# Inverse and chain of a recurrence, by group of four heads, in a hybrid attention layer

## The chip, the core and the metric

The kernel runs on one core of a Trainium2 chip. The metric is the device time of one execution in microseconds. A core has TensorE (PE, with its weight loads PEld), VectorE (DVE), ScalarE (ACT), GpSimd (POOL) and SyncE (SP), which here only issues DMAs. Each engine works through its own list of instructions strictly in order and waits where a semaphore isn't there yet.

## The reference

One layer, D_MODEL 1024, 1024 positions. A normed input is multiplied with `w_in`; the product is split into a part for latent attention (4 heads), a part for an RWKV-7 recurrence (8 heads of 64) and a gate z. Cut to the recurrence:

```python
def step(S, inp):
    r_t, w_t, k_t, v_t, kk_t, a_t = inp
    sa = jnp.einsum('bhvk,bhk->bhv', S, -kk_t)
    S = (S * w_t[:, :, None, :] + sa[..., None] * (kk_t * a_t)[:, :, None, :]
         + v_t[..., None] * k_t[:, :, None, :])
    return S, jnp.einsum('bhvk,bhk->bhv', S, r_t)
...
_, ys = lax.scan(step, S0, xs)
y = jnp.moveaxis(ys, 0, 1)          # then a group norm per head, scale, bias and a bonus term
...
y_cat = jnp.concatenate([y_mla, y_rw], axis=-1) * jax.nn.silu(z)
h = h + rmsnorm(y_cat @ w_out[l], norm_post_g[l])
```

## The kernel before

The positions go in two halves h of 512, and a half in 8 chunks (NCH) of 64 for the recurrence. Within a chunk the recurrence is written with matrices: a head needs the inverse of a 64 x 64 unit triangular matrix per chunk, and then a chain of small matmuls carries the state from chunk to chunk. The heads form two groups g of four; cb counts pairs of heads (128 columns), so that blocks 0 and 1 belong to group 0, and 2 and 3 to group 1.

A string, PROGRAM, lists the stages. A letter is a stage, its digits are the half and the block or group:

- A: load x, norm it, transpose it and split it into uH and uL (L181 scales, L188 transposes, L192 and L193 split). X: the inputs of the low-rank weights.
- P h cb: projections r, k, v (L221, with weights split by L201 on ScalarE and L209 or L211 on GpSimd), and the factors of the recurrence (L322 and L329 write LS).
- E h cb: the unit matrices (L372, masked by L376 and L377 into AB and LS; L386, L399, L407).
- I: the inverse. C: the chain. N and G: group norm and outputs (L522 to L542).
- Z, Y: projections of the gate z (also L221, L602), stored to zs. M, T: attention's input. B: rope tables. U, K, J, Q, S: attention and the output product (L814 and L862 scores, L894, L942 output).

The stages are written in this order. A scheduler then places every instruction in its engine's list by a model of the times; buffers in rotation (`ch` 2, `wk` 2 and `pj` 4 in PSUM; AB, LS, BK and SV one per group, shared by both halves) and data set the waits. BEHIND holds X0 and B back until the named stage's last instruction.

The inverse of a half works on 128 blocks of 32 x 32 (two groups, four heads, two diagonal blocks, eight chunks), one on each partition. The unit matrices go to `sa` in DRAM (L395) and come back block by partition (L423). For each of 31 columns two VectorE instructions (L430, L432) eliminate, up to 256 elements wide. The inverse and its transpose (L433) go out by two stores (L434, L435) and come back in the matmuls' layout by 20 loads (L442, L446, L449). Two small matmul stages fill the off-diagonal block (pF at L459, pG at L466, copied by L460, L467, L468).

The chain takes 8 steps a half, each for both groups: matmuls L486 (state times LS), L497 (inverse), L503 (new state) and L493 and L509 (output), with copies L488, L499 and L513 on ScalarE, L500 and the sum L506 on VectorE, and the decayed state SD (L490) on GpSimd.

Of the kernel before, what the change touches and what calls it, by code (L numbers as in the profile page):

```python
# [12 lines left out]
ALU = mybir.AluOpType  # L13
# [8 lines left out]
NCH = HALF // CH  # L22
# [23 lines left out]
def layer(tc, x, pos, w_in, w_out, w_uq, w_ukv, vecs, w2, a2, consts, post_g, out):  # L46
# [17 lines left out]
    with tc.tile_pool(name="sb", bufs=1) as cp, \  # L64
# [65 lines left out]


PROGRAM = (
    "A0 X0 Z00 P00 E00 Z01 P01 E01 Z02 P02 E02 P03 E03 I0 C0 N00 G00 N01 G01 M0 Z03 Z04 Z05 Y06 T0 A1 B X1",
    "P10 E10 Z10 P11 E11 Z11 P12 E12 P13 E13 I1 C1 N10 G10 N11 G11 M1 Z12 T1 Z13 Z14 Z15 Z16 Z17 U K J Q0",
    "Q1 Q2 Q3 S",
)


BEHIND = {"X0": "A0", "B": "I0"}


def recurrence(tc, E):
    nc = tc.nc
    V, S, G, PE, SP = nc.vector, nc.scalar, nc.gpsimd, nc.tensor, nc.sync
    alloc, bc = E["alloc"], E["bc"]
    vec, omm, oka, hka, nkk, hwa, hln, plast, Sst = (
        E[k] for k in ("vec", "omm", "oka", "hka", "nkk", "hwa", "hln", "plast", "Sst"))
# [4 lines left out]
    P1, pj, wk, chp = E["cp"], E["pj"], E["wk"], E["chp"]  # L152
# [4 lines left out]
    ev = (slice(0, 64), slice(64, 128))  # L157
    le = [(l, e) for l in range(2) for e in range(2)]
# [251 lines left out]
        S.copy(SV[0:64, 0::2, 1, :], pv[0:64, :, 64:128])  # L410
        V.tensor_copy(SV[0:64, 1::2, 1, :], pv[64:128, :, 64:128])

    def inverse(h, gt):


        sa = gt["sa"]
        sx = alloc(E["dp"], (2, 2, 2, 2, NCH, 32, 32), f"sx{h}")
        st = alloc(E["dp"], (2, 2, 2, 2, NCH, 32, 32), f"st{h}")
        rows = "g e b l c i j -> (g e b l c) i j"
        XA = alloc(P1, (128, 2, 1024), "XA")  # L420
        X = XA[:, 0].rearrange("p (i c) -> p i c", c=32)
        At = XA[:, 1].rearrange("p (i c) -> p i c", c=32)
        SP.dma_start(At, sa.rearrange(rows))  # L423
        G.memset(XA[:, 0], 0.0)
        G.memset(XA[:, 0, 0::33], 1.0)
        for j in range(31):
            n, w = 31 - j, j + 1
            tmp = alloc(P1, (128, 256), "tmp")
            t3 = tmp[:, 0:n * w].rearrange("p (n w) -> p n w", w=w)
            V.tensor_tensor(t3, bc(At[:, j, j + 1:32].unsqueeze(2), (128, n, w)),  # L430
                            bc(X[:, j, 0:w].unsqueeze(1), (128, n, w)), ALU.mult)
            V.tensor_tensor(X[:, j + 1:32, 0:w], X[:, j + 1:32, 0:w], t3, ALU.add)  # L432
        V.tensor_copy(At, X.rearrange("p i c -> p c i"))  # L433
        SP.dma_start(sx.rearrange(rows), X)  # L434
        SP.dma_start(st.rearrange(rows), At)  # L435
        FX = alloc(P1, (128, 2, 4, NCH, 32), "XA")
        for g in range(2):
            AB = gt["g"][g]["AB"]
            X1, X2T = FX[:, g, 0:2], FX[:, g, 2]
            for e in range(2):  # L440
                p0 = e * 64
                SP.dma_start(X1[p0:p0 + 32].rearrange("p l c j -> p (l c) j"),  # L442
                             sx[g, e, 0].rearrange("l c i j -> i (l c) j"))
                for l in range(2):
                    q = l * 2 + e
                    SP.dma_start(X2T[q * 32:q * 32 + 32], st[g, e, 1, l].rearrange("c i j -> i c j"))  # L446
                for b in range(2):
                    p0 = e * 64 + b * 32
                    SP.dma_start(AB[p0:p0 + 32, :, :, b * 32:b * 32 + 32].rearrange("p l c j -> p (l c) j"),  # L449
                                 st[g, e, b].rearrange("l c i j -> i (l c) j"))  # L450
        for g in range(2):
            AB = gt["g"][g]["AB"]
            X1, X2T, F = FX[:, g, 0:2], FX[:, g, 2], FX[:, g, 3]
            pF = chp((128, NCH, 32))
            for c in range(NCH):
                for l, e in le:
                    q = l * 2 + e
                    r = slice(e * 64, e * 64 + 32)
                    PE.matmul(pF[q * 32:q * 32 + 32, c], AB[r, l, c, 32:64], X1[r, l, c], start=True, stop=True)  # L459
            V.tensor_copy(F, pF)  # L460
            for l in range(2):
                pG = chp((128, NCH, 32))
                for c in range(NCH):
                    for e in range(2):
                        q = slice((l * 2 + e) * 32, (l * 2 + e) * 32 + 32)
                        PE.matmul(pG[e * 64:e * 64 + 32, c], F[q, c], X2T[q, c], start=True, stop=True)  # L466
                end = V.tensor_copy(AB[0:32, l, :, 32:64], pG[0:32])  # L467
                S.copy(AB[64:96, l, :, 32:64], pG[64:96])  # L468
        return end

    def chain(h, gt):

        for g in range(2):
            for e in range(2):
                G.tensor_copy(gt["g"][g]["SV"][ev[e], 0, e], Sst[ev[e], 2 * g:2 * g + 2])
        parts = [tuple(gt["g"][g][k] for k in ("LS", "BK", "AB", "SV")) +
                 (Sst[:, 2 * g:2 * g + 2], gt["Dg"][:, 2 * g:2 * g + 2]) for g in range(2)]
        for c in range(NCH):

            pY = wk((128, 2, 2, 64))  # L480
            pcs = [chp((128, 3, 2, 64)) for _ in range(2)]
            Rs = [alloc(P1, (128, 2, 64), "Rs", bufs=2) for _ in range(2)]
            SD = [alloc(P1, (128, 2, 64), "SD", bufs=2) for _ in range(2)]
            for (LS, BK, AB, SV, St, Dg), pc, R_, D_ in zip(parts, pcs, Rs, SD):
                for l, e in le:
                    PE.matmul(pc[ev[e], 0, l], LS[:, l, c, e, 0:64], SV[:, c, e, l], start=(l == 0), stop=False,  # L486
                              skip_group_check=True)
                S.copy(R_, pc[:, 0])  # L488
                for e in range(2):
                    G.tensor_tensor(D_[ev[e]], SV[ev[e], c, e], bc(Dg[ev[e], :, c:c + 1], (64, 2, 64)), ALU.mult)  # L490
            for g, (LS, BK, AB, SV, St, Dg) in enumerate(parts):
                for l, e in le:
                    PE.matmul(pY[ev[e], g, l], LS[:, l, c, e, 64:128], SV[:, c, e, l], start=(g == 0 and l == 0), stop=False,  # L493
                              skip_group_check=True)
            for (LS, BK, AB, SV, St, Dg), pc, R_ in zip(parts, pcs, Rs):
                for l, e in le:
                    PE.matmul(pc[ev[e], 1, l], AB[ev[e], l, c, 0:64], R_[ev[e], l], start=False, stop=False,  # L497
                              skip_group_check=True)
                S.copy(SV[ev[0], c, 0], pc[ev[0], 1])  # L499
                V.tensor_copy(SV[ev[1], c, 1], pc[ev[1], 1])  # L500
            for (LS, BK, AB, SV, St, Dg), pc, D_ in zip(parts, pcs, SD):
                for l, e in le:
                    PE.matmul(pc[ev[e], 2, l], BK[:, l, c, e], SV[:, c, e, l], start=False, stop=True, skip_group_check=True)  # L503
                for e in range(2):
                    dst = SV[ev[e], c + 1, e] if c + 1 < NCH else St[ev[e]]
                    V.tensor_tensor(dst, pc[ev[e], 2], D_[ev[e]], ALU.add)  # L506
# [102 lines left out]
    lora, xx, gts, cqs, made = {}, {}, {}, {}, {}  # L609
# [29 lines left out]
def attention(tc, E):  # L639
# [92 lines left out]
    def op_k():  # L732
# [348 lines left out]
```

## Time and profile before

| | |
|---|---|
| three runs | 775.58, 780.02, 776.13 us; median 776.13 |
| profiled execution | 775.78 us |
| its span in the trace | 772.4 us |
| TensorE busy | 689.6 us (89%) |
| VectorE busy | 454.0 us (59%) |
| ScalarE, GpSimd busy | 345.8 us (45%), 331.1 us (43%) |
| mean granted clock of TensorE | 0.933 |

The profile page gives busy times, 40 slices of the span with the busy share of each engine and the granted clock in tenths, the DMA queues, the chain of work that ended last, and the costliest groups of instructions with the idle time before them and what ended it. Times in it are of one execution.

### The profile page before, as it was taken

Reading aid. Unit: us, or ns where it says so; the run is one execution under the profiler, and the core shown is the slowest. Engines: PE = TensorE matmul, PEld = TensorE weight load, DVE = VectorE, ACT = ScalarE, POOL = GpSimd, SP = SyncE. Lnnn points to the kernel's source line nnn. Section 1 sums busy time; section 2 is a strip of 40 time slices with the busy share of each in tenths; the row PEclk is TensorE's granted clock in tenths of the full one; section 3 lists DMA queues with packets and bytes.
Section 4 is the critical chain, followed back from the end, with each engine's and each line's share of the span. In section 5 each row is a group of like instructions: output and inputs, shape, how many; then the busy total and the mean of one; then the engine's idle time right before and its main releaser. Section 6 shows DMA issues by size and latency. Waiting matters only on the chain.

```text
span 772.4 us, 13874 instructions
## 1 busy us (share of the span) xinstructions
PE 689.6 (89%) x5136; PEld 564.9 (73%) x5136; DVE 454.0 (59%) x943; ACT 345.8 (45%) x875; POOL 331.1 (43%) x478
## 2 busy tenths in 40 slices
PE   2899998999858999859899989498899999899996
PEld 2677786787746777647778867386789988788885
DVE  4466675639829431684755593486777776644233
ACT  6646544428225452524634532332665475632221
POOL 6656555447712455453463652132512247432220
PEclk9899999999958899958999999598999999999998
DMA  6523332543570132252222554501231044253321
GB/s 185 150 80 89 91 81 65 145 122 100 167 158 19 28 109 58 55 116 60 54 68 72 138 157 124 164 15 30 57 75 49 22 126 121 72 169 121 123 81 55
DMA packets 118819, 72.84 MB, mean 94 GB/s; under 512 B 47072, under 2 KB 108256, under 8 KB 118752
## 3 DMA queue, kind: packets, MB, share of 16 engines
q1 hardware_dynamic: 118752, 71.96, 33.2%
q8 instruction: 40, 0.66, 0.3%
q14 instruction: 27, 0.22, 0.1%
HBM read 54.38 MB, written 17.56 MB: 93 GB/s over the span
## 4 chain that ended last, share of the span: by engine, by line
PE 36%; DVE 12%; DMA 4%; ACT 3%; POOL 2%; issue 2%; SPq 2%; DVEq 0%; ACTq 0%; POOLq 0%
PE pj L942 11%; PE pj L221 5%; PE pj L862 4%; PE ch L894 3%; DVE tmp L430 2%; PE pj L814 2%; DVE XA L432 2%; PE wk L883 2%; PE wk L372 1%; PE ch L503 1%; POOL w L211 1%; PE wk L509 1%; ACT wf L870 1%; PE pj L821 1%; DMA XA<-sa 1%
## 5 line engine op out<-in xcount | busy, mean ns | idle before, releaser
L221 PE MATMUL pj<-uH,w 128*128 128x512 f32 x640 | 214.9, 409 | 5.7 <-ACT sg L289 4.8
L211 POOL TENSOR_TENSOR w<-wf,w 128x256 fp32r<-128x256 f32 x168 | 140.0, 864 | 117.9 <-ACT w L201 106.8
L221 PEld LDWEIGHTS pj<-uH,w 128*128 128x128 f32 x640 | 121.8, 193 | 36.1 <-ACT sg L289 5.4
L221 PE MATMUL pj<-uL,w 128*128 128x512 f32 x320 | 129.4, 405 | 0.0
L221 PEld LDWEIGHTS pj<-uL,w 128*128 128x128 f32 x320 | 61.8, 193 | 14.2 <-issue 1.2
L201 ACT CAST w<-wf 128x1024 fp32r<-128x1024 f32 (+1 forms) x50 | 51.3, 1027 | 35.9 <-PE pj L556 17.3
L490 POOL TENSOR_TENSOR SD<-SV,Dg 64x128 f32<-64x128 f32 x64 | 30.0, 468 | 57.2 <-DVE SV L506 47.8
L874 POOL TENSOR_SCALAR wf<-wf,sm 128x128 f32<-128x128 f32 (+7 forms) x32 | 23.8, 747 | 62.2 <-DVE sm L873 45.4
L999 DVE TENSOR_TENSOR LS<-pj,LS 128x512 f32<-128x512 f32 x16 | 11.1, 691 | 45.1 <-ACT cq L998 44.4
L430 DVE TENSOR_TENSOR tmp<-XA 128x31 f32<-128x31 f32 (+15 forms) x62 | 28.1, 454 | 15.1 <-DMA XA<-sa 13.3
L885 ACT CAST BK<-wk 128x512 fp32r<-128x512 f32 (+3 forms) x48 | 22.6, 484 | 29.2 <-PE wk L883 27.4
L894 PE MATMUL ch<-BK,LS 128*128 128x256 f32 (+1 forms) x160 | 33.0, 288 | 0.2 <-ACT BK L885 0.2
L209 POOL TENSOR_TENSOR w<-wf,w 128x224 fp32r<-128x224 f32 x32 | 22.1, 722 | 25.5 <-ACT w L201 15.4
L886 DVE TENSOR_TENSOR AB<-wk,BK 128x512 fp32r<-128x512 f32 (+3 forms) x48 | 26.1, 551 | 8.5 <-ACT BK L885 8.1
L865 DVE TENSOR_REDUCE mx<-pj 128x1 f32<-128x512 f32 (+3 forms) x48 | 26.0, 552 | 8.5 <-PE pj L864 5.6
L870 ACT ACTIVATE wf<-pj,mx 128x512 f32<-128x512 f32 (+3 forms) x48 | 27.9, 588 | 5.2 <-DVE mx L867 5.0
L432 DVE TENSOR_TENSOR XA<-XA,tmp 128x31 f32<-128x31 f32 (+15 forms) x62 | 27.5, 443 | 1.9
L372 PEld LDWEIGHTS wk<-LS,pl 64*128 64x128 f32 x256 | 19.3, 187 | 12.2 <-issue 11.2
L998 ACT ACTIVATE cq<-pj 128x512 bf16<-128x512 f32 x16 | 9.6, 597 | 41.1 <-PE pj L942 41.1
L894 PEld LDWEIGHTS ch<-BK,LS 128*128 128x128 f32 x160 | 26.8, 197 | 0.9 <-ACT BK L885 0.5
L513 ACT COPY SV<-wk 128x128 f32<-128x128 f32 x32 | 6.9, 269 | 45.6 <-PE wk L509 45.6
L372 PE MATMUL wk<-LS,pl 64*128 64x128 f32 x256 | 24.8, 290 | 2.7 <-DVE LS L377 2.3
(337 smaller groups left out, 1668.2 us busy)
## 6 DMA issues: line engine op xcount, KB each, us to landing
wf<-in_w_in_dram SPq DMA_DIRECT2D x42, 512.0 KB, 3.8
zs<-st SPq DMA_DIRECT2D x16, 256.0 KB, 2.5
wf<-in_x_dram SPq DMA_DIRECT2D x8, 512.0 KB, 3.7
out_dram<-LS SPq DMA_DIRECT2D x16, 256.0 KB, 2.0
wf<-in_w_in_dram SPq DMA_DIRECT2D x8, 448.0 KB, 3.5
bvd<-st SPq DMA_DIRECT2D x8, 256.0 KB, 2.0
SV<-bvd SPq DMA_DIRECT2D x16, 128.0 KB, 2.9
yrw<-SV SPq DMA_DIRECT2D x8, 256.0 KB, 3.1
```

The source lines that it names most:

```text
L201: S.copy(wh, wf)
L211: G.tensor_tensor(wl[:, sl], wf[:, sl], wh[:, sl].bitcast(F32), ALU.subtract)
L221: PE.matmul(ps, w_[:, kb], u_[:, kb], start=(n == 0), stop=(n == 23))
L372: PE.matmul(pE[e][:, ci], pl[ev[e], c4 + ci, 1 - e:3 - e].rearrange("p a b -> p (a b)"), LS[ev[e], c4 + ci, e, :], start=True, stop=True)
L430: V.tensor_tensor(t3, bc(At[:, j, j + 1:32].unsqueeze(2), (128, n, w)), bc(X[:, j, 0:w].unsqueeze(1), (128, n, w)), ALU.mult)
L432: V.tensor_tensor(X[:, j + 1:32, 0:w], X[:, j + 1:32, 0:w], t3, ALU.add)
L490: G.tensor_tensor(D_[ev[e]], SV[ev[e], c, e], bc(Dg[ev[e], :, c:c + 1], (64, 2, 64)), ALU.mult)
L862: PE.matmul(s_, l_, r_, start=(n == 0), stop=(n == 4 and b1 < e))
L870: S.activation(pr[:, b0:b1], sc[:, 0:b1 - b0], AF.Exp, bias=mx[:, 0:1], scale=-1.0, accum_out=sm[:, n5:n5 + 1])
L886: V.tensor_tensor(PL[:, b0:b0 + nb, o], pt[:, 0:nb], PH[:, b0:b0 + nb, o].bitcast(F32), ALU.subtract)
L894: PE.matmul(py[:, o], l_, r_, start=(j == 0 and n == 0), stop=(j == nk - 1 and n == 2), skip_group_check=True)
L942: PE.matmul(po[nb], l_, r_[:, ns], start=(k0 == 0 and k == 0 and n == 0), stop=(k0 == 4 and k == 3 and n == 2), skip_group_check=True)
```

## The change

Inverse and chain become stages of a group. I h g follows the group's second block of unit matrices, and C h g follows it; some z projections move between the blocks.

The inverse of a group has only 64 blocks. Each is put on two partitions, one on each half of the 128: the lower 64 hold the even columns of X and the upper 64 the odd ones. A column j then touches w = j // 2 + 1 columns at most on each partition, instead of j + 1. There are 62 elimination instructions per group (L432, L434), so 124 a half, up to 136 elements wide. A group has two loads of `sa` (L425), four stores (L437, L438) and 12 loads (L444, L448, L451). The chain has 16 steps a half, each of one group, and its pY now comes from the `ch` buffers instead of `wk`. After the change pF stands at L458, pG at L466, the chain's matmuls at L482, L490, L493, L498 and L503, SD at L488, its VectorE copy at L496 and sum at L501.

```diff
-    "A0 X0 Z00 P00 E00 Z01 P01 E01 Z02 P02 E02 P03 E03 I0 C0 N00 G00 N01 G01 M0 Z03 Z04 Z05 Y06 T0 A1 B X1",
-    "P10 E10 Z10 P11 E11 Z11 P12 E12 P13 E13 I1 C1 N10 G10 N11 G11 M1 Z12 T1 Z13 Z14 Z15 Z16 Z17 U K J Q0",
+    "A0 X0 Z00 P00 E00 P01 E01 I00 C00 Z01 P02 E02 Z02 P03 E03 N00 G00 I01 C01 N01 G01 M0 Z03 Z04 Z05 Y06 T0 A1 B X1",
+    "P10 E10 Z10 P11 E11 I10 C10 Z11 P12 E12 Z12 P13 E13 N10 G10 I11 C11 N11 G11 M1 Z13 T1 Z14 Z15 Z16 Z17 U K J Q0",
...
-BEHIND = {"X0": "A0", "B": "I0"}
+BEHIND = {"X0": "A0", "B": "I01"}
...
-    def inverse(h, gt):
-        sa = gt["sa"]
-        sx = alloc(E["dp"], (2, 2, 2, 2, NCH, 32, 32), f"sx{h}")
-        XA = alloc(P1, (128, 2, 1024), "XA")
...
-        SP.dma_start(At, sa.rearrange(rows))
+    def inverse(h, g, gt):
+        AB = gt["g"][g]["AB"]
+        sx = alloc(E["dp"], (2, 2, 2, 2, NCH, 32, 16), f"sx{h}{g}")
+        st = alloc(E["dp"], (2, 2, 2, NCH, 16, 2, 32), f"st{h}{g}")
+        XA = alloc(P1, (128, 2048), "XA")
+        X = XA[:, 0:512].rearrange("p (i k) -> p i k", k=16)
+        Xt = XA[:, 512:1024].rearrange("p (k i) -> p k i", i=32)
+        At = XA[:, 1024:2048].rearrange("p (j t) -> p j t", t=32)
+        G.memset(XA[:, 0:512], 0.0)
+        for o in range(2):
+            SP.dma_start(At[ev[o]], gt["sa"][g].rearrange("e b l c j t -> (e b l c) j t"))
+            G.memset(XA[ev[o], 16 * o:512:33], 1.0)
         for j in range(31):
-            n, w = 31 - j, j + 1
+            n, w = 31 - j, j // 2 + 1
...
-        SP.dma_start(sx.rearrange(rows), X)
-        SP.dma_start(st.rearrange(rows), At)
+        V.tensor_copy(Xt, X.rearrange("p i k -> p k i"))
+        for o in range(2):
+            SP.dma_start(st[:, :, :, :, :, o].rearrange("e b l c k i -> (e b l c) k i"), Xt[ev[o]])
+            SP.dma_start(sx[o].rearrange("e b l c i k -> (e b l c) i k"), X[ev[o]])
...
-    def chain(h, gt):
-        for g in range(2):
-            for e in range(2):
-                G.tensor_copy(gt["g"][g]["SV"][ev[e], 0, e], Sst[ev[e], 2 * g:2 * g + 2])
+    def chain(h, g, gt):
+        for e in range(2):
+            G.tensor_copy(SV[ev[e], 0, e], St[ev[e]])
         for c in range(NCH):
-            pY = wk((128, 2, 2, 64))
-            pcs = [chp((128, 3, 2, 64)) for _ in range(2)]
+            pc = chp((128, 3, 2, 64))
+            pY = chp((128, 2, 64))
...
-        "E": op_e, "I": lambda h: inverse(h, gts[h]), "C": lambda h: chain(h, gts[h]),
+        "E": op_e, "I": lambda h, g: inverse(h, g, gts[h]), "C": lambda h, g: chain(h, g, gts[h]),
```

What the scheduler makes of it is seen in the engines' lists. Before, VectorE's list has the chain's first step of half 0 behind the whole inverse and among the rope tables and A1's split; from the last elimination on, with pF's and pG's copies between:

```order
L430 TENSOR_TENSOR tmp_262_1503<-XA_231_1409 128x31
L432 TENSOR_TENSOR XA_231_1409<-XA_231_1409,tmp_262_1503 128x31
L433 COPY XA_231_1409<-XA_231_1409 128x1024
L193 SCALAR_TENSOR_TENSOR uL_20_99<-pj_398_2730,vec_2_65,uH_19_98 128x256 x2
L460 COPY XA_263_1509<-ch_264_1530 128x256
L193 SCALAR_TENSOR_TENSOR uL_20_99<-pj_399_2739,vec_2_65,uH_19_98 128x256
L467 COPY AB_65_323<-ch_265_1564 32x8x32
```

After, VectorE's list at the first step of group 0's chain in half 0; SV_66 and ch_185 are group 0's state and its step, the rows of XA_304 are group 1's inverse, and BK_68 is a unit matrix of E03:

```order
L496 COPY SV_66_324<-ch_185_1026 64x128
L432 TENSOR_TENSOR tmp_305_1902<-XA_304_1896 128x31
L434 TENSOR_TENSOR XA_304_1896<-XA_304_1896,tmp_305_1902 128x31
L432 TENSOR_TENSOR tmp_306_1905<-XA_304_1896 128x30
L434 TENSOR_TENSOR XA_304_1896<-XA_304_1896,tmp_306_1905 128x30
...
L432 TENSOR_TENSOR tmp_309_1914<-XA_304_1896 128x81
L501 TENSOR_TENSOR SV_66_324<-ch_185_1026,SD_188_1034 64x128 x2
L434 TENSOR_TENSOR XA_304_1896<-XA_304_1896,tmp_309_1914 128x27x5
```

The chain's copy and its sum, which stood behind the inverse, now stand in the middle of the next one, four and a half pairs of eliminations apart.

On TensorE, before, E03's unit matrices (wk_219 and wk_220) follow P03's projections directly:

```order
L372 MATMUL wk_219_1330<-LS_67_325,pl_203_1217 128x128
L372 MATMUL wk_220_1331<-LS_67_325,pl_203_1217 128x128
L372 MATMUL wk_219_1330<-LS_67_325,pl_203_1217 128x128
L372 MATMUL wk_220_1331<-LS_67_325,pl_203_1217 128x128
L372 MATMUL wk_219_1330<-LS_67_325,pl_203_1217 128x128
```

After, the same unit matrices (wk_289 and wk_290) in the middle of M0 (L547 to L549); ch_182 is pF of group 0's inverse:

```order
L548 MATMUL pj_376_2382<-w_380_2387,uH_19_98 128x448
L549 MATMUL pj_376_2382<-w_380_2387,uL_20_99 128x448
L372 MATMUL wk_289_1779<-LS_67_325,pl_273_1666 128x128
L458 MATMUL ch_182_952<-XA_181_939,AB_65_323 32x32 x31
L372 MATMUL wk_290_1780<-LS_67_325,pl_273_1666 128x128
L372 MATMUL wk_289_1779<-LS_67_325,pl_273_1666 128x128
L372 MATMUL wk_290_1780<-LS_67_325,pl_273_1666 128x128
```

pF's 32 matmuls (one of them stands earlier, in P03's last projection), which followed A1's transposes, now stand ahead of all but the first of E03's unit matrices.

More of the change, by code (lines that the diff above doesn't have):

```diff
@@ L451, in inverse @@
[L451 to L463, printed above, removed]
-                    for e in range(2):
[L465 to L468, printed above, removed]
@@ new lines, in inverse @@
+        V.tensor_copy(Xt, X.rearrange("p i k -> p k i"))
+        for o in range(2):
+            SP.dma_start(st[:, :, :, :, :, o].rearrange("e b l c k i -> (e b l c) k i"), Xt[ev[o]])
+            SP.dma_start(sx[o].rearrange("e b l c i k -> (e b l c) i k"), X[ev[o]])
+        FX = alloc(P1, (128, 4, NCH, 32), "XA")
+        X1, X2T, F = FX[:, 0:2], FX[:, 2], FX[:, 3]
+        for e in range(2):
+            p0 = e * 64
+            for o in range(2):
+                SP.dma_start(X1[p0:p0 + 32].rearrange("p l c j -> p (l c) j")[:, :, 16 * o:16 * o + 16],
+                             sx[o, e, 0].rearrange("l c i k -> i (l c) k"))
+            for l in range(2):
+                q = l * 2 + e
+                SP.dma_start(X2T[q * 32:q * 32 + 32], st[e, 1, l].rearrange("c k o i -> (k o) c i"))
+            for b in range(2):
+                p0 = e * 64 + b * 32
+                SP.dma_start(AB[p0:p0 + 32, :, :, b * 32:b * 32 + 32].rearrange("p l c j -> p (l c) j"),
+                             st[e, b].rearrange("l c k o i -> (k o) (l c) i"))
@@ new lines, in inverse @@
+        pF = chp((128, NCH, 32))
+        for c in range(NCH):
+            for l, e in le:
+                q = l * 2 + e
+                r = slice(e * 64, e * 64 + 32)
+                PE.matmul(pF[q * 32:q * 32 + 32, c], AB[r, l, c, 32:64], X1[r, l, c], start=True, stop=True)
+        V.tensor_copy(F.rearrange("p c (k o) -> p c o k", o=2), pF.rearrange("p c (o k) -> p c o k", o=2))
+        for l in range(2):
+            pG = chp((128, NCH, 32))
+            for c in range(NCH):
+                for e in range(2):
+                    q = slice((l * 2 + e) * 32, (l * 2 + e) * 32 + 32)
+                    PE.matmul(pG[e * 64:e * 64 + 32, c], F[q, c], X2T[q, c], start=True, stop=True)
+            end = V.tensor_copy(AB[0:32, l, :, 32:64], pG[0:32])
+            S.copy(AB[64:96, l, :, 32:64], pG[64:96])
@@ new lines, in inverse @@
+        return end
+    def chain(h, g, gt):
+        LS, BK, AB, SV = (gt["g"][g][k] for k in ("LS", "BK", "AB", "SV"))
+        St, Dg = Sst[:, 2 * g:2 * g + 2], gt["Dg"][:, 2 * g:2 * g + 2]
+        for e in range(2):
+            G.tensor_copy(SV[ev[e], 0, e], St[ev[e]])
+        for c in range(NCH):
+            pc = chp((128, 3, 2, 64))
+            pY = chp((128, 2, 64))
+            for l, e in le:
+                PE.matmul(pc[ev[e], 0, l], LS[:, l, c, e, 0:64], SV[:, c, e, l], start=(l == 0), stop=False,
+                          skip_group_check=True)
+            Rs = alloc(P1, (128, 2, 64), "Rs", bufs=2)
+            S.copy(Rs, pc[:, 0])
+            SD = alloc(P1, (128, 2, 64), "SD", bufs=2)
+            for e in range(2):
+                G.tensor_tensor(SD[ev[e]], SV[ev[e], c, e], bc(Dg[ev[e], :, c:c + 1], (64, 2, 64)), ALU.mult)
+            for l, e in le:
+                PE.matmul(pY[ev[e], l], LS[:, l, c, e, 64:128], SV[:, c, e, l], start=(l == 0), stop=False,
+                          skip_group_check=True)
+            for l, e in le:
+                PE.matmul(pc[ev[e], 1, l], AB[ev[e], l, c, 0:64], Rs[ev[e], l], start=False, stop=False,
+                          skip_group_check=True)
+            S.copy(SV[ev[0], c, 0], pc[ev[0], 1])
+            V.tensor_copy(SV[ev[1], c, 1], pc[ev[1], 1])
+            for l, e in le:
+                PE.matmul(pc[ev[e], 2, l], BK[:, l, c, e], SV[:, c, e, l], start=False, stop=True, skip_group_check=True)
+            for e in range(2):
+                dst = SV[ev[e], c + 1, e] if c + 1 < NCH else St[ev[e]]
+                V.tensor_tensor(dst, pc[ev[e], 2], SD[ev[e]], ALU.add)
+            for l, e in le:
+                PE.matmul(pY[ev[e], l], AB[ev[e], l, c, 64:128], SV[ev[e], c, e, l], start=False, stop=True,
+                          skip_group_check=True)
+            S.copy(SV[:, c, 0], pY)
```

56 lines of the change are left out of this document (removed).

## The prediction

> **What bounds the kernel now.** I read the page from the top: the busy shares, then the slices of TensorE and its clock, then a table of stretches cut at the hollow slices, and last the waits inside these.
>
> ```profile
> span 772.4 us, 13874 instructions
> PE 689.6 (89%) x5136; PEld 564.9 (73%) x5136; DVE 454.0 (59%) x943; ACT 345.8 (45%) x875; POOL 331.1 (43%) x478
> PE   2899998999858999859899989498899999899996
> PEclk9899999999958899958999999598999999999998
> ```
>
> TensorE bounds the kernel on average, but not everywhere. Three slices have both a low busy digit and a clock digit of 5, and they fall where the inverse and chain of a half begin or end. The table of stretches prices them. Its columns are the window and its length, then for TensorE, its weight loads, VectorE, ScalarE and GpSimd the busy time with the count, then the granted clock.
>
> ```profile
> core 0: us, PE busy (x) PEld busy (x) DVE busy (x) ACT busy (x) POOL busy (x), PEclk, DMA share, GB/s
> 63.00:119.40 56.40, 56.40 (x325) 44.52 (x324) 39.23 (x56) 28.19 (x56) 32.18 (x46) 1.00 0.34 87
> 209.00:256.00 47.00, 33.54 (x469) 25.65 (x468) 25.89 (x69) 18.44 (x47) 14.13 (x23) 0.68 0.42 108
> 324.00:352.00 28.00, 16.63 (x111) 13.94 (x108) 23.20 (x38) 9.44 (x24) 16.89 (x19) 0.57 0.47 109
> 352.00:411.00 59.00, 56.48 (x333) 44.67 (x332) 37.17 (x55) 26.21 (x53) 26.82 (x36) 0.97 0.24 63
> 411.00:482.00 71.00, 67.58 (x455) 54.98 (x456) 41.65 (x89) 27.64 (x71) 33.86 (x51) 0.98 0.46 126
> 482.00:506.00 24.00, 13.68 (x233) 9.94 (x225) 12.75 (x30) 7.95 (x24) 5.41 (x10) 0.57 0.52 147
> 531.00:561.00 30.00, 25.20 (x355) 20.90 (x355) 19.46 (x51) 15.35 (x55) 11.79 (x16) 0.89 0.23 54
> ```
>
> I take as lost what is left of a stretch after busy time times clock, as an estimate: 47 − 33.5 × 0.68 = 24.2 us at the end of half 0, 28 − 16.6 × 0.57 = 18.5 us in half 1's first block, 24 − 13.7 × 0.57 = 16.2 us at half 1's inverse, and 30 − 25.2 × 0.89 = 7.6 us at the end of its chain. Together 66.5 us. The first row is the opposite: over two blocks of projections and unit matrices (P01 to E02, with two z projections) TensorE stood still nowhere, and VectorE was busy 39.2 of 56.4 us. It has 17 us to spare there, and that is the room into which the change puts half an inverse.
>
> What do the hollow stretches wait for? The inverse's DMA round trip, as SyncE's queue shows (start, duration of the issue, line):
>
> ```profile
> 164.10 2.14 SPq L395 DMA_DIRECT2D sa<-AB  x4
> 167.54 0.34 SPq L423 DMA_DIRECT2D XA<-sa  x1
> ...
> 210.15 0.33 SPq L435 DMA_DIRECT2D st<-XA  x1
> 212.84 0.32 SPq L442 DMA_DIRECT2D XA<-sx  x1
> 223.13 0.98 SPq L449 DMA_DIRECT2D AB<-st  x2
> ...
> 483.07 0.97 SPq L449 DMA_DIRECT2D AB<-st  x2
> 484.14 0.91 SPq L589 DMA_DIRECT2D zs<-st  x2
> 488.57 1.81 SPq L713 DMA_DIRECT2D cq<-cTd  x4
> ```
>
> Then how long L449's loads take to land, and TensorE's longest waits of the whole run (total, times, longest):
>
> ```profile
> DMA to landing us min/median/max: 2.2/2.4/4.3
> ```
>
> ```profile
> PE pj L188 <- DVE v L181: 10.5, 1, 10.5
> PE ch L486 <- ACT AB L468: 8.7, 3, 7.8
> PE ch L459 <- DMA XA<-sx: 8.6, 3, 5.2
> ```
>
> The inverse's last store is issued at 210.15, the first load 2.7 us later, and the last of the 20 loads goes out near 224, at about 0.5 us each, and lands 2.4 us later: some 16 us in which no chain step can run. At half 0's end no projection is left to fill it, so pF (L459) and the first step (L486) show up as TensorE's longest waits, beside the start of the kernel. In half 1 the same loads end at 484, and the z store and the query phase's loads (L713) stand behind them on SyncE.
>
> **What the change removes.** Group 0's inverse and chain start two blocks earlier, so that at half 0's end only the last steps of group 0 and group 1's start remain. The waits of 24.2 us go, since A1's transposes and X1 now stand beside a chain that already runs. In half 1, P10 writes the tiles LS and BK of group 0, and those were free only after the common chain and its group norm; now group 0's chain ends right behind X1. Group 1's buffers are wanted by P12, two blocks later. So the 18.5 us go as well. At half 1's end, 20 loads become 12 and only group 1's are late; of the 16.2 us I leave 12 (below, half of it, 8, as 12 loads are little more than half of 20; above, all of it), because the z store and L713 still stand behind them. The 7.6 us at the chain's end turn into a dense end of group 1's chain.
>
> **What it adds: VectorE.** The two groups of the first inverse, and behind them single answers on L430 (durations min/median/max) for the whole run and for two moments, and on GpSimd's L211:
>
> ```profile
> L430 DVE TENSOR_TENSOR tmp<-XA 128x31 f32<-128x31 f32 (+15 forms) x31 | 14.1, 455 | 7.5 <-DMA XA<-sa 6.7
> L432 DVE TENSOR_TENSOR XA<-XA,tmp 128x31 f32<-128x31 f32 (+15 forms) x31 | 13.8, 445 | 1.0
> ```
>
> ```profile
> L430 DVE TENSOR_TENSOR tmp<-XA x62: 191/389/920, 172.8 to 468.4; 128x31 f32<-128x31 f32 x4, 128x60 f32<-128x60 f32 x4, 128x87 f32<-128x87 f32 x4, 128x112 f32<-128x112 f32 x4
> L430 DVE TENSOR_TENSOR tmp<-XA x1: 417/417/417, 450.6 to 450.6; 128x256 f32<-128x256 f32 x1
> L430 DVE TENSOR_TENSOR tmp<-XA x1: 673/673/673, 207.2 to 207.2; 128x31 f32<-128x31 f32 x1
> L211 POOL TENSOR_TENSOR w<-wf,w x31: 722/867/1179, 123.7 to 208.5; 128x256 fp32r<-128x256 f32 x31
> ```
>
> 31 elements take 191 ns and 256 take 417: 160 ns and 1.0 ns an element. The 31 columns hold 5456 elements in each of the two lines, so 62 instructions should take 62 × 0.16 + 2 × 5.46 = 20.8 us; they took 14.1 + 13.8 = 27.9. The 7 us between are instructions of the kind of the fifth row, 673 ns for the same 31 elements. They run beside L211, GpSimd's weight subtraction (722 to 1179 ns), and cost about 0.48 us more each; 7 us is some 15 of the 62. After the change a group has the same 62 instructions with 2856 elements a line: 62 × 0.16 + 2 × 2.86 = 15.6 us, and two groups 31.3. So halving the width with twice the instructions costs 10.5 us a half before any contention. With 15 held instructions a group, it is 2 × 22.6 = 45.2 us against 27.9, **17.3 us more VectorE per half**; with 24 held, some 9 us more still.
>
> The Trainium skill (SBUF — State Buffer, section "Who interferes with whom") says that a VectorE instruction with two SBUF inputs and a GpSimd instruction that reads SBUF take turns on one port pair, whole instruction by whole instruction. This speaks against the change: the price of being held would hang on the count of instructions and not on their width. The two rows for 31 elements, 191 and 673 ns, agree. If width set the price instead, the held part would halve, and the sum would be 7 us a half lower.
>
> **Where that falls.** In the stretch from P02 to E03, VectorE has 39.2 us of blocks, 22.6 us of inverse and some of group 0's chain copies (three a step, 0.3 us each by the chain's rows below, so 7 us for eight steps): 62 to 69 us against TensorE's 56.4. VectorE is late by 6 to 13 us; I take 12, near the upper end, since the inverse also waits for its own load (6.7 us before, in the row of L430), and what VectorE has to do in that time is not all ready. From here on, order decides who pays, because every engine works strictly in its order:
>
> - pF's matmuls (L458) stand ahead of E03's unit matrices in TensorE's order. They wait for VectorE's copy, four stores and twelve loads, by the queue above 2.7 + 12 × 0.5 + 2.4 = 11 us. Below, it costs 0 where M0's matmuls ahead of it last as long; I take 4, since VectorE's lateness is in part the same wait.
> - Group 0's chain copies (L496, L501) stand among group 1's inverse on VectorE, L501 of the first step behind five pairs that wait for the inverse's load. Below, only the five pairs are in the way, 2.5 us; above, the load's 6.7, those pairs and three more us for the second step, 12. I take 8, as the load's wait has a row and is the nearest.
> - Group 1's chain of half 0 runs its first two steps without a projection between them, beside the rope tables' instructions on VectorE, and P10 to E11 run with it. Below, two lone steps at 1.3 us each (worked out below), 2.6; above, the whole 18.5 us again. I take 10, between them.
> - Half 1's first inverse stands among P12 and E12, with P12's LS writes behind nearly all of it: as in half 0, but 59 − 56.5 × 0.97 = 4.2 us were lost there already. From 0 to the 12 of half 0; I take 6.
> - Group 1's inverse of half 1 stands among M1 and the last z projections, with group 0's chain: from 0 to the 12 of half 0's second inverse; I take 5, since five z projections are left to fill.
>
> **What it adds: chain steps.** The chain's step of both groups, by VectorE's instructions at the dense place:
>
> ```profile
> 305.69 0.53 DVE L500 COPY SV<-ch 64x128 f32<-64x128 f32 x2 [5.45 <-issue]
> 306.54 0.61 DVE L506 TENSOR_TENSOR SV<-ch,SD 64x128 f32<-64x128 f32 x2 [0.32 <-PE ch L503]
> 307.30 0.61 DVE L506 TENSOR_TENSOR SV<-ch,SD 64x128 f32<-64x128 f32 x2 [0.15 <-PE ch L503]
> 309.57 0.57 DVE L500 COPY SV<-ch 64x128 f32<-64x128 f32 x2 [1.67 <-POOL SD L490]
> ```
>
> 309.57 − 305.69 = 3.9 us for both groups. A step of one group has half the matmuls but the same string of matmul, copy, matmul, copy, matmul, add; it takes between 1.95 and 3.9 us, and I take 3.2, nearer to the whole, for the string sets it. Sixteen such steps a half replace eight. Beside projections this costs nothing; where a step stands alone, it is 3.2 − 1.95 = 1.3 us of standing TensorE. Group 1's last steps of half 1 stand alone: 4 to 8 steps, 5 us (0 where attention's first scores fill them; 8 × 1.3 = 10 above). GpSimd's product SD stands in its queue ahead of later weight subtractions as before.
>
> **The sum.** Costs 12 + 4 + 8 + 10 + 6 + (12 + 5) + 5 = 62 us against 66.5 us: 4.5 us less. The profiled execution took 775.78 us, 3.4 us over its span of 772.4 and 0.35 below the median of 776.13. So 772.4 − 4.5 + 3.4 = 771, and I say **770 us**. All lower ends (6, 0, 2.5, 2.6, 0, 8, 0) sum to 19 and give 728; all upper ends (13, 11, 12, 18.5, 12, 28, 10) sum to 104.5 and give 814; nobody should expect all of one side at once. A difference under 1% (7.8 us) is about what can't be told from no change.
>
> **Rivals.**
>
> Faster: VectorE's slack carries the inverse. For it speaks the first row of the stretches, 17 us to spare in 56, and that TensorE fell behind in no block of half 0. If lateness, pF and the chain behind the inverse cost 10 instead of 24, and P10 to E13 10 instead of 16, 20 us come off: 750, from 735 to 760. Chance 0.27.
>
> Slower: VectorE becomes the bound of P02 to E03 and P12 to E13. It decides where VectorE's work there passes TensorE's 56.4 us by over about 14 us, that is with 24 or more held instructions a group: 9 us more in each half, and the chain, whose copies queue behind the inverse, adds the 4 us up to its upper end in each half. That is 770 + 18 + 8 = 796, from 784 to 806. For it speaks that L211 runs all through the projections, 31 times in the 90 us to 209. Against it: L211 is idle for much of that, waiting for its casts. Chance 0.27.
>
> No effect: group 1's chain still sets when P12 may write, as the common chain did for P10; the half's hollow only moves two blocks on. Then the 18.5 us stay, and some of the 10 go: 776, within 1%. Chance 0.04.
>
> The forecast's own case, 760 to 783, has 0.42: 0.16 faster by over 1%, 0.22 within, 0.04 slower. That makes 0.43 faster, 0.26 within 1%, 0.31 slower. The range leaves out the outer parts of both rivals: 742 to 797.
>
> **What would show it.** The hollow slices with clock 5 near 210 to 256 and 324 to 352 should be gone. In L432 and L434 I expect x124 each, a mean near 0.35 us, and executions of 31 elements at both 0.2 and 0.65 us. VectorE's sum should be near 454 + 35 = 489 us, TensorE's matmul count unchanged. A wait of TensorE's L458 for DMA in M0, and of L372 or L221 behind it, would confirm the pF step; waits of L498 or L503 for VectorE's L496 and L501 the chain step. The forecast is wrong if the new inverse instructions are held far more or less often than 15 in 62, or if the query phase near 485 no longer waits for SyncE's queue.

## The result, and the profile after

The changed kernel takes 800.7 us (median of four runs, 799.06 to 804.02) against 775.9 us for the kernel before: a ratio of 1.029, with a 95% interval from 1.024 to 1.034. It is slower by 25 us by the medians and the two profiles (797.8 against 772.4 us of span), by 22 us by the ratio, whose interval is 19 to 26. The forecast was 770 us, and the range ended at 797.

The head of the page after, with the slices of TensorE and its clock:

```profile
span 797.8 us, 14046 instructions
PE 716.9 (90%) x5136; PEld 579.0 (73%) x5136; DVE 488.4 (61%) x1069; ACT 349.4 (44%) x878; POOL 322.7 (40%) x486
PE   3889989799988969999999989869888997899996
PEclk9999999999997968998999989678779999899999
```

At first sight TensorE is busier than before, 90%, with the same 5136 matmuls, and still takes longer. Its busy time grew by 27 us. That can't be work; it is the same matmuls at a lower clock or pulled apart. The clock row reads 6, 7, 8, 7, 7 in the 26th to the 30th slice, 499 to 598 us, where the row before read 5, 9, 8, 9, 9.

The table of stretches, first at the windows of the prediction, then where the second head's scores end and the third's begin (columns as before: window, length, TensorE, its loads, VectorE, ScalarE, GpSimd, clock):

```profile
209.00:256.00 47.00, 41.83 (x385) 34.28 (x383) 18.44 (x42) 20.10 (x48) 19.99 (x35) 0.92 0.48 118
324.00:352.00 28.00, 28.00 (x197) 20.97 (x196) 19.45 (x29) 15.20 (x36) 16.02 (x23) 1.00 0.30 80
560.00:616.30 56.30, 49.29 (x411) 40.81 (x411) 28.93 (x76) 20.23 (x61) 14.06 (x21) 0.79 0.14 36
566.40:585.00 18.60, 14.95 (x190) 11.73 (x190) 5.12 (x16) 5.33 (x18) 3.99 (x10) 0.59 0.01 2
```

The two hollows of the prediction are gone: 41.8 of 47 us busy at a clock of 0.92, and 28.0 of 28 at 1.00. What is new is the last row: 18.6 us in which VectorE, ScalarE and GpSimd are busy for 4 to 5 us each, the DMA engines rest, and TensorE's mean clock is 0.59. From the first matmul of the second head's projection (L807) to that of the third's, the kernel takes 616.3 − 560.0 = 56.3 us. Before, the same piece (L814 there) took 25.7 us without a gap:

```profile
567.00:592.70 25.70, 25.70 (x172) 23.32 (x171) 19.21 (x53) 14.60 (x42) 5.92 (x8) 1.00 0.18 47
```

To find out where the loss arises although the order of the work changed, I gave each matmul the distance at which its kind follows itself at full clock in the trace before (230 ns for L221, for example), added these up in TensorE's order, and took the sum from the time at which a stage begins. What is left is the lag: everything but work. The distances are rough. Before, the piece from the second to the third head's projection has no gap and a clock of 1.00, and yet its lag falls by 3.5 us; differences of 3 us mean little.

| stage begins | before: time, lag | after: time, lag | lag after − before |
|---|---|---|---|
| M0 | 149.6, 20.9 | 159.4, 30.7 | +9.8 |
| T0 | 208.1, 22.7 | 229.1, 39.0 | +16.3 |
| P10 | 252.4, 48.3 | 259.1, 51.7 | +3.4 |
| P12 | 357.3, 81.7 | 348.4, 74.3 | −7.4 |
| M1 | 411.5, 83.9 | 421.7, 87.7 | +3.8 |
| first head's projection | 497.8, 104.9 | 507.2, 108.6 | +3.7 |
| second head's projection | 567.0, 132.4 | 560.0, 131.2 | −1.2 |
| third head's projection | 592.7, 128.9 | 616.3, 152.6 | +23.7 |
| output product | 674.4, 129.8 | 699.9, 155.4 | +25.6 |

At the second head's projection the two kernels are level, after gains and losses of up to 16 us on the way. The loss that stays comes in one place, between the second and the third. What TensorE does there is seen in its timeline (start, duration, line, count, idle time before it and what ended it):

```profile
566.29 0.44 PE L503 MATMUL ch<-SV,AB 64*64 64x64 f32 x6
567.14 0.45 PE L482 MATMUL ch<-SV,LS 128*64 128x64 f32 x8 [0.41 <-ACT SV L506]
...
570.65 0.69 PE L482 MATMUL ch<-SV,LS 128*64 128x64 f32 x8 [0.41 <-ACT SV L506]
571.13 0.64 PE L490 MATMUL ch<-SV,LS 128*64 128x64 f32 x8
571.71 0.69 PE L493 MATMUL ch<-Rs,AB 64*64 64x64 f32 x8
572.82 0.47 PE L503 MATMUL ch<-SV,AB 64*64 64x64 f32 x2 [0.41 <-ACT SV L495]
573.22 0.69 PE L498 MATMUL ch<-SV,BK 128*64 128x64 f32 x8
573.85 0.69 PE L503 MATMUL ch<-SV,AB 64*64 64x64 f32 x6
574.72 0.70 PE L482 MATMUL ch<-SV,LS 128*64 128x64 f32 x8 [0.19 <-DVE SV L501]
...
582.84 0.70 PE L482 MATMUL ch<-SV,LS 128*64 128x64 f32 x8 [0.18 <-DVE SV L501]
583.89 0.69 PE L493 MATMUL ch<-Rs,AB 64*64 64x64 f32 x8
585.38 0.79 PE L855 MATMUL pj<-w,w 128*128 128x512 f32 x1 [0.79 <-DVE LS L810]
```

These are steps of group 1's chain of half 1, one behind the other, and nothing between them. The first takes 570.65 − 567.14 = 3.5 us, later ones 582.84 − 574.72 over two = 4.1 us, at half clock. As its last matmul on LS (L490) is done, at 584.0 us, ScalarE and VectorE write LS for attention (L809, L810), and the scores go on: attention uses LS, AB, BK and SV of the groups again and had to wait for group 1's. Its mixing (L887) draws on `ch` too, and comes at 603 us, behind the group norm. Group 1's chain ends at 592 us; before, the common chain ended at 550.

The reason it ends so late is read from the starts of pF, which opens each chain: 157, 276, 412 and 533 us, and from the starts of each chain's last matmuls on the state: 258, 395, 523 and 592. Each pF stands behind the chain ahead of it. Half 1's second inverse was finished on VectorE by 473 us, and its pF waited until 533, behind the other group's chain and its outputs. So there are 32 steps in one string where there were 16, at 5 to 25 us a step while other work stands between, and about 4 where none is left.

### The profile page after: what moved, and what is told of

Its sections match the earlier page's. It is cut to its first block, busy times and chain, and to the rows that moved or that the text cites. A ratio compares the mean times of both kernels' runs of the same rounds, so it can differ in the third digit from the quotient of the medians.

```text
span 797.8 us, 14046 instructions
## 1 busy us (share of the span) xinstructions
PE 716.9 (90%) x5136; PEld 579.0 (73%) x5136; DVE 488.4 (61%) x1069; ACT 349.4 (44%) x878; POOL 322.7 (40%) x486
## 4 chain that ended last, share of the span: by engine, by line
PE 58%; DVE 24%; ACT 7%; DMA 6%; issue 4%; POOL 1%; SPq 1%; DVEq 0%; ACTq 0%; POOLq 0%
PE pj L221 17%; PE pj L935 11%; PE pj L855 4%; PE ch L887 3%; DVE tmp L432 3%; DVE XA L434 3%; PE ch L503 2%; PE pj L807 2%; PE wk L372 2%; PE wk L876 2%; PE pj L595 2%; PE ch L498 1%; DVE AB L376 1%; DVE LS L322 1%; PE pj L547 1%
## 5 line engine op out<-in xcount | busy, mean ns | idle before, releaser
L221 PE MATMUL pj<-uH,w 128*128 128x512 f32 x640 | 219.1, 415 | 3.4 <-ACT sg L289 2.5
L211 POOL TENSOR_TENSOR w<-wf,w 128x256 fp32r<-128x256 f32 x168 | 134.9, 834 | 87.2 <-ACT w L201 68.3
L221 PEld LDWEIGHTS pj<-uH,w 128*128 128x128 f32 x640 | 123.7, 195 | 34.2 <-ACT sg L289 2.7
L221 PE MATMUL pj<-uL,w 128*128 128x512 f32 x320 | 131.0, 410 | 0.0
L488 POOL TENSOR_TENSOR SD<-SV,Dg 64x128 f32<-64x128 f32 x64 | 27.5, 429 | 126.8 <-DVE SV L501 121.4
L221 PEld LDWEIGHTS pj<-uL,w 128*128 128x128 f32 x320 | 62.9, 196 | 15.4 <-issue 1.8
L867 POOL TENSOR_SCALAR wf<-wf,sm 128x128 f32<-128x128 f32 (+7 forms) x32 | 24.9, 781 | 68.1 <-DVE sm L866 54.1
L432 DVE TENSOR_TENSOR tmp<-XA 128x126 f32<-128x126 f32 (+22 forms) x124 | 42.6, 344 | 13.4 <-DMA XA<-sa 10.0
L434 DVE TENSOR_TENSOR XA<-XA,tmp 128x126 f32<-128x126 f32 (+22 forms) x124 | 42.0, 339 | 3.9
L506 ACT COPY SV<-ch 128x128 f32<-128x128 f32 x32 | 8.6, 270 | 64.2 <-PE ch L503 64.2
L887 PE MATMUL ch<-BK,LS 128*128 128x256 f32 (+1 forms) x160 | 34.4, 299 | 1.5 <-DVE SV L535 0.8
L501 DVE TENSOR_TENSOR SV<-ch,SD 64x128 f32<-64x128 f32 x56 | 16.2, 289 | 30.0 <-PE ch L498 28.7
L503 PE MATMUL ch<-SV,AB 64*64 64x64 f32 x256 | 28.8, 270 | 5.0 <-ACT SV L495 5.0
L496 DVE COPY SV<-ch 64x128 f32<-64x128 f32 x32 | 9.4, 295 | 37.8 <-ACT SV L495 36.0
L887 PEld LDWEIGHTS ch<-BK,LS 128*128 128x128 f32 x160 | 28.1, 207 | 2.5 <-ACT BK L878 1.2
```

Of the source, the lines that this page charges most:

```text
L211: G.tensor_tensor(wl[:, sl], wf[:, sl], wh[:, sl].bitcast(F32), ALU.subtract)
L221: PE.matmul(ps, w_[:, kb], u_[:, kb], start=(n == 0), stop=(n == 23))
L488: G.tensor_tensor(SD[ev[e]], SV[ev[e], c, e], bc(Dg[ev[e], :, c:c + 1], (64, 2, 64)), ALU.mult)
L503: PE.matmul(pY[ev[e], l], AB[ev[e], l, c, 64:128], SV[ev[e], c, e, l], start=False, stop=True, skip_group_check=True)
L887: PE.matmul(py[:, o], l_, r_, start=(j == 0 and n == 0), stop=(j == nk - 1 and n == 2), skip_group_check=True)
```

## The experiments

Theory S says just that: the chains are in series, and the string of steps is what half 1's end waits for. Theory V says that VectorE's longer inverse is the cause. Ratios are against the kernel before on the same chip, where it took 777 to 780 us, with 95% intervals.

**Which half.** One kernel has half 0 by group and half 1 as before (the cut shows its line of half 0), another the reverse:

```diff
-    "A0 X0 Z00 P00 E00 Z01 P01 E01 Z02 P02 E02 P03 E03 I0 C0 N00 G00 N01 G01 M0 ...",
+    "A0 X0 Z00 P00 E00 P01 E01 I00 C00 Z01 P02 E02 Z02 P03 E03 N00 G00 I01 C01 N01 G01 M0 ...",
```

> Half 0 by group as in the changed kernel; half 1 with the inverse and the chain of the kernel before, in its order. Theory S (the chains are in series: with two chains a half instead of one, the last one ends at 592 us instead of 546, its last steps stand alone at half clock, and attention waits for its buffers): half 1's chain is again one string of eight steps, so the loss behind the second head's scores goes, 20 to 26 us of the 25, and what half 0 gained by P12 (7 us) shows: 768 to 778 us. Theory V (VectorE's 17 us more a half): half of the loss goes, 786 to 792 us.

> The other half: half 0 with inverse and chain of the kernel before, half 1 by group. Theory S: the last chain is still two in series behind half 0's common chain, 795 to 805 us. Theory V: half of the loss, 786 to 792 us.

Half 0 alone by group: 782.7 us, ratio 1.005 (1.002 to 1.008). Half 1 alone by group: 805.9 us, 1.034 (1.028 to 1.039), just over the upper end of S. Half 1 costs all of it that is clear of noise, and half 0 by group gains nothing. In lag, the piece between the second and the third head's projection costs −3.5 us with half 1 as before (138.4 to 134.9; before itself 132.4 to 128.9), and +20.2 with half 1 by group (140.0 to 160.2). This speaks for S; V expected an even share, 786 to 792 us for both, and neither is. The time of the first kernel missed S's 768 to 778, since the 7 us that half 0 gains by P12 are lost again by the first head's projection (lag 108.9 against 104.9).

**Without the eliminations.** In both kernels the loop over columns is cut to its first column; the rest of the elimination is left out.

```diff
-        for j in range(31):
+        for j in range(1):
```

> The changed kernel with one column of elimination instead of 31 in each of the four inverses; 240 VectorE instructions and some 82 us of VectorE are left out, all else stays. Theory V: the loss goes, 765 to 777 us or below. Theory S: the chains stay in series, so 785 to 800 us, and the last chain's lone steps stay.

> The kernel before with one column of elimination instead of 31 in both inverses (120 VectorE instructions, some 54 us, left out), as the partner of the run without eliminations of the changed kernel. At the ends of both halves the elimination lies on the path, so it gets faster: 735 to 760 us. Theory S: it stays 20 us or more ahead of its partner. Theory V: the two come within 8 us of each other.

778.5 us and 758.1 us. The first lies between the ranges of the two theories, and the second in its own. Without nearly all of their 83 or 55 us of eliminations, the changed kernel is still 20.4 us behind its partner, as S asked, where it was 24.9 behind with them. By these medians VectorE's added elimination explains 4.5 us of the 25. By the ratios (0.999 and 0.973, against 1.029) it is some 2, and their intervals reach from nothing to about 9. Between the second and third projection the changed kernel without eliminations loses 19.3 us of lag (112.5 to 131.8), its partner gains 3.8.

**The chain alone.** This kernel is the kernel before with its order and its inverses; half 1's chain goes group by group. With it pY moves from `wk` to `ch` in that half, as in the changed kernel, so the run tests the two together.

```diff
-    "... P13 E13 I1 C1 N10 G10 N11 G11 ...",
+    "... P13 E13 I1 C10 C11 N10 G10 N11 G11 ...",
```

> The kernel before, order and inverses included, with one thing changed: in half 1 the chain runs group by group, group 0's eight steps and then group 1's, instead of both groups in each step. VectorE's inverse is that of before. Theory S: the string of 16 steps alone costs what half 1 by group costs, 12 to 30 us: 788 to 806 us, with the loss behind the second head's scores. Theory V, or any theory in which the inverse's place matters: within 8 us of before, 772 to 788 us.

801.1 us, ratio 1.029 (1.025 to 1.032): in S's range, and the same ratio as for the whole change. The timeline shows the same lone steps (lines are moved by the two versions in one file, L482 is the step's first matmul, L958 the scores):

```profile
564.76 0.45 PE L482 MATMUL ch<-SV,LS 128*64 128x64 f32 x8 [0.41 <-ACT SV L506]
568.51 0.70 PE L482 MATMUL ch<-SV,LS 128*64 128x64 f32 x8 [0.19 <-DVE SV L501]
572.57 0.70 PE L482 MATMUL ch<-SV,LS 128*64 128x64 f32 x8 [0.19 <-DVE SV L501]
576.63 0.70 PE L482 MATMUL ch<-SV,LS 128*64 128x64 f32 x8 [0.19 <-DVE SV L501]
...
587.29 1.65 PE L958 MATMUL pj<-w,w 128*128 128x512 f32 x3 [0.79 <-DVE LS L913]
```

A step of one group alone takes 4.06 us, 572.57 − 568.51, at half clock; the one at full clock in the changed kernel took 3.5. Before, a step of both groups took 3.9 at full clock. Half the work takes nearly as long, so the split nearly doubles the string's length. The two groups in one step had hidden each other's waits: of two and a half such steps of the kernel before, with no other work on TensorE from 303.4 us on, it is busy for 8.90 of 9.60 us:

```profile
303.00:312.60 9.60, 8.90 (x193) 7.30 (x192) 3.80 (x13) 4.13 (x15) 5.53 (x12) 1.00 0.23 60
```

**The inverse alone.** Inverses by group at the places of the change, but one common chain a half (the cut shows half 0, against the changed kernel; half 1 is written alike).

```diff
-    "... I00 C00 Z01 P02 E02 Z02 P03 E03 N00 G00 I01 C01 N01 G01 M0 ...",
+    "... I00 Z01 P02 E02 Z02 P03 E03 I01 C0 N00 G00 N01 G01 M0 ...",
```

> The changed kernel's inverse by group in both halves and at its places, but one chain a half with both groups in each step, behind the second group's inverse. Theory S: the loss behind the second head's scores is gone, and only half an inverse stands at each half's end: 755 to 778 us. Theory V: VectorE has the same added work as in the changed kernel, so 790 to 800 us.

791.8 us, ratio 1.018 (1.014 to 1.022). S missed here, and V's range holds it. The loss sits elsewhere, though: the piece behind the second projection is as before (lag 150.9 to 147.4), and the lag at M1 is 104.3 us against 83.9. So with a common chain the inverse by group costs some 20 us by M1. In the changed kernel, which has the same inverses at the same places, the lag at M1 is 87.7; that its early chains make up for them is read from these two lags and was not tested by itself. The two parts don't add up to the change, 14 and 22 us against 22 by the ratios; how the inverse's part splits between VectorE's time and its order was not tried.

**Fewer steps.** Five of the eight steps of one of half 1's chains are left out, their outputs set to zero.

```diff
+        if (h, g) == (1, 1):
+            G.memset(SV[:, 3:, 0], 0.0)
-        for c in range(NCH):
+        for c in range(3 if (h, g) == (1, 1) else NCH):
```

> The changed kernel with only three of the eight steps in the last chain (half 1, group 1); five steps are left out and their outputs set to zero, everything else stays. In the changed kernel five of these steps stood alone between 566 and 584 us. Theory S: a step that stands alone costs all of its 4.1 us, so five cost 17 to 24 us: 777 to 784 us. If only TensorE's standing time counted, as the prediction had it (1.3 us a step): 793 to 797 us.

> The same with the chain ahead of it: only three of eight steps of half 1's group 0, whose steps stood among M1, T1 and the z projections at some 13 us each. If the two chains are one string that sets the end, as theory S has it, leaving out five of its steps lets group 1's chain start up to 60 us earlier, beside projections, and the lone steps go: 775 to 788 us, much as with the last chain's. If a covered step is free and only the last ones count: 796 to 802 us.

767.7 us (0.985, 0.980 to 0.991) without five steps of the last chain, and 773.0 us (0.992, 0.989 to 0.996) without five of the chain ahead of it. Against the ratio of 1.029 both give back 28 to 34 us, that is 5.7 to 6.8 us a step, and both lie below S's ranges. A part of it is the work of the 200 matmuls that go with five steps. That the first chain's steps, which stood among projections, give back almost as much as the last chain's is what a string does, and no sum of standing times: an earlier start of the last chain lets it run beside projections.

**The cover moved.** Four z projections are held back until the first chain of half 1 has ended.

```diff
-BEHIND = {"X0": "A0", "B": "I01"}
+BEHIND = {"X0": "A0", "B": "I01", "Z14": "C10", "Z15": "C10", "Z16": "C10", "Z17": "C10"}
```

> The changed kernel with the z projections Z14 to Z17 held back until the last step of half 1's first chain (C10). That takes the cover from this chain and leaves the projections to the gap before the last chain. In TensorE's order five steps of C10 now stand alone instead of five of C11, and the last chain stands among attention's first work. If a step costs its whole 4 us wherever it stands alone, and the string of 16 steps only moves: 795 to 806 us. If what costs is only that the last chain ends late and holds attention's buffers: it now ends some 20 us earlier, 780 to 790 us.

796.3 us, ratio 1.026 (1.019 to 1.032): little moved, as the first view expected and not the second. Now four of the first chain's steps stand alone, from 478 to 494 us, at the same 4.06 us; two windows of this kernel, its lone steps and then the place where they stood:

```profile
472.00:495.00 23.00, 18.53 (x190) 14.42 (x188) 8.39 (x26) 6.14 (x19) 4.74 (x12) 0.50 0.45 94
566.00:585.00 19.00, 17.61 (x156) 13.85 (x156) 9.92 (x30) 7.83 (x26) 3.68 (x7) 1.00 0.00 1
```

Where the lone steps stand makes no clear difference: the last chain ended 7 us earlier (585 against 592), and the two ratios, 1.026 and 1.029, lie within each other's intervals.

**Order of the norm, and the buffer of pY.** Both are attempts on the two `ch` buffers. In the first, group 0's norm and outputs come behind group 1's chain, in both halves (the cut shows half 1); in the second, pY goes back to `wk`.

```diff
-    "... N10 G10 I11 C11 N11 G11 M1 ...",
+    "... I11 C11 N10 G10 N11 G11 M1 ...",
...
-            pY = chp((128, 2, 64))
+            pY = wk((128, 2, 64))
```

> The changed kernel with group 0's group norm and outputs written behind group 1's chain in both halves. pF, pG, the chain and the outputs draw on the two buffers ch in the order of writing, so group 1's pF need no longer wait for group 0's norm. In half 1 this wait was 516 (last step of group 0) to 533 us. Theory S: group 1's last chain ends 8 to 16 us earlier, and the time falls by 4 to 14 us: 787 to 797. Without the buffers mattering: 800 us, within 4.

> The changed kernel with the chain's output sums pY in the buffers wk, as before, instead of ch. Rival theory B: the chain's two ch buffers, shared by pc and pY, slow each step, so that 8 us or more come back: below 792 us. Theory S gives no gain from it: a step's string is the same, and wk is wanted by the unit matrices, which now must wait for the chain or go ahead of it: 796 to 815 us.

816.7 us (1.049, 1.044 to 1.053) and 865.9 us (1.112, 1.109 to 1.114). The first was a miss for both views. In half 1 the wait aimed at did go: pF starts 1.3 us behind the last matmuls on the state of the chain ahead (550.6 to 551.9), where it had been 10 us (523 to 533). The loss had come before. SV of group 0 stays taken until its outputs are done, and these now come at 372 to 383 us in half 0 instead of 269. Half 1's first block, whose matmuls for SV (L407) were done by 311.5, can copy them (L409, L411) only at 381 to 383, and holds a buffer of `wk` until then, so that the unit matrices wait:

```profile
372.00:418.40 46.40, 25.37 (x155) 20.78 (x154) 33.79 (x75) 12.60 (x29) 7.49 (x14) 0.56 0.23 55
```

In the second, pY shares `wk` with the unit matrices, whose buffers go round in the order of writing. The next block's unit matrices can't pass the chain, and the steps stand alone already in the first chain: from 162 to 186 us its matmuls on the state start 4 us apart, seven in a row. Both ranges end far below 865.9 us; S's 815 left out most of what holding back the unit matrices costs. That pY moved to `ch` was needed. Rival B falls: with pY out of `ch` a lone step at half clock still takes 4.0 us.

**A better use of the z projections.** The kernel before with two of half 0's z projections written behind M0, and with two of half 1's as well.

> The kernel before with the z projections Z01 and Z02 of half 0 written behind M0 instead of among the first blocks, nothing else. They are 11 us of TensorE that could stand in the wait for the inverse at 209 to 236 us. If the first blocks don't need them to cover VectorE (39.2 us of 56.4 in two blocks), 4 to 11 us faster: 765 to 773. If they do, TensorE stands earlier instead: 772 to 782 us.

> The same in both halves: Z10 and Z11 also stand behind M1, where they can cover the inverse's loads at 482 to 495 us. By the same two views 755 to 770, or 772 to 785 us.

776.8 us, ratio 0.997 (0.994 to 1.000), and 783.4 us, 1.007 (1.003 to 1.010). In the first, the lag at P10 falls from 48.3 to 44.6 and half 1 takes it back (81.7 and 82.1 at P12). Both lie in the range of the second view, that the first blocks need these projections. Nothing here is clearly faster than the kernel before.

## Why the prediction was wrong

Step by step, in the lag that each stretch adds, after against before:

| stretch | predicted | measured |
|---|---|---|
| start to P10 | −24.2 + 12 + 4 + 8 = −0.2 | +3.4 |
| P10 to P12 | −18.5 + 10 = −8.5 | −10.8 |
| P12 to M1 | +6 | +11.2 |
| M1 to the first head's projection | −16.2 + 12 + 5 = +0.8 | −0.1 |
| from there to the end | −7.6 + 5 = −2.6 | +21.9 |
| sum | −4.5 | +25.6 |

- **The gains held.** The hollows at 209 to 256 and 324 to 352 us are gone, for the reasons given: group 0's chain runs ahead of A1 and beside it, and P10 finds its buffers free. From 482 to 506 us TensorE is busy for 20.8 of 24 us at 0.90, where it was busy for 13.7 at 0.57.
- **VectorE held, in part by luck.** Its sum was to be 489 us and is 488.4, but the eliminations were 5.8 us below the forecast and the rest of VectorE's work, forecast as unchanged, 5.4 us above. Behind the blocks it was to make TensorE late by 12 us, pF by 4 more and the chain behind the inverse by 8; the lag, after less before, was 9.8 at M0 and 16.3 at T0. From P12 to M1 it grew by 11.2 us instead of 6. The groups of the new inverse, from the page:

```profile
L432 DVE TENSOR_TENSOR tmp<-XA 128x126 f32<-128x126 f32 (+22 forms) x124 | 42.6, 344 | 13.4 <-DMA XA<-sa 10.0
L434 DVE TENSOR_TENSOR XA<-XA,tmp 128x126 f32<-128x126 f32 (+22 forms) x124 | 42.0, 339 | 3.9
```

  They sum to 84.6 us, where four times 22.6 = 90.4 were expected and the same two rows of before sum to 55.6. Over all single instructions, 50 of the 248 stand more than 0.15 us above the line through the free ones, by 0.42 us on average; before it was 30 of 124, by 0.44. Before, every one of the 30 overlaps a weight subtraction of GpSimd (L211). The price of a held instruction did not fall with the halved width, as the prediction had concluded from the page that it weighed (the Trainium skill, SBUF — State Buffer, "Who interferes with whom"); here the trace agrees. The share that is held was 12.5 in 62, near the 15 expected.
- **The waits that were named are there but small.** From TensorE's list of waits (total, times, longest):

```profile
PE ch L498 <- DVE SV L496: 5.2, 5, 1.7
PE ch L503 <- ACT SV L495: 5.0, 10, 0.8
PE ch L482 <- DVE SV L501: 3.6, 5, 2.8
PE ch L458 <- DMA XA<-sx: 3.3, 1, 3.3
```

- **The step that failed is the chain's price at the end.** The prediction had it that where a step stands alone only TensorE's standing time counts, 3.2 − 1.95 = 1.3 us, and gave the last steps 5 us in all; from the second to the third head's projection alone the lag grew by 24.9 us more than before, and the run with the chain alone cost 22 us. Two things are wrong in it. First, the size: a lone step takes 3.5 us at full clock and 4.06 at the half to which it fell, and no other work goes on meanwhile. By the prediction's own measure, busy time times clock, the lone steps lose 18.60 − 14.95 × 0.59 = 9.8 us, some 2 us each, and the whole piece 56.30 − 49.29 × 0.79 = 17.4 us, for attention's work stands late behind them. Second, I priced the chains stage by stage and never added them up. By the prediction's own numbers the split lengthens a half's string from 8 × 3.9 = 31 to 16 × 3.2 = 51 us. With `ch` handed on in the order of writing, the last chain stood behind group 0's chain and outputs: its pF started at 533 us, and without the eliminations still at 512. Attention's scores waited for its last reads of LS at 584 us; before, the whole common chain had ended at 550. "Beside projections this costs nothing" was the sentence that hid it: a covered step costs TensorE nothing, but it makes the last chain late.
- **The slower rival came true in its size, but not by its mechanism.** Its 784 to 806 us held the time, yet it made VectorE the bound. In the changed kernel the runs without eliminations leave VectorE some 2 to 5 of the 25 us; only with a common chain does the inverse by group cost 14 us by itself. No rival spoke of the chain's length.

## What to carry to other kernels

Two independent strings of dependent steps that run in one loop hid each other's waits here; split into two loops, they ran one behind the other, and what set the end was the count of steps times a step's latency. No run gave the second chain buffers of its own, so how much of the series is due to the buffers and how much to the order of writing stays open. Before splitting such a loop, add up the whole string from its first start to what waits for its end, buffers handed on included, and compare that with the work that is there to cover it. A gain at the hollows that the profile shows must be weighed against that sum, not only against the waits around the edit.

## What the runs showed of the hardware

The granted clock, the share of full speed that TensorE is given, fell to one half while TensorE counted as busy most of the time. In 566.4 to 585.0 us of the changed kernel TensorE is listed as busy for 14.95 of 18.60 us, and the mean clock is 0.59; with the cover moved, 18.53 of 23.00 us and 0.50. The matmuls there move 64 columns and have tiles of 128 x 64 or 64 x 64; in that kernel's window from 566 to 585, with scores of 512 columns between the steps, 17.61 of 19.00 us are busy at a clock of 1.00. I had taken a low clock as a sign of standing. A stretch of small matmuls can have it while it is listed as busy for 80%, and part of the 27 us by which TensorE's busy time grew is this. The size alone does not explain it: the kernel before's steps of both groups, some 190 matmuls of the same sizes in 9.60 us, are busy for 8.90 us and run at 1.00, where the 190 of the lone steps are spread over 18.60 us. What the clock goes by instead, no run here shows.
